# Two groups' norm sums a bunch later, a fourth raw-weight buffer, a split interval and a reordered opening in a hybrid decoder trunk

## The chip, the core and the metric

The kernel runs on one core of one Trainium2 chip. The metric is the device time of one execution in microseconds (us). Three executions of the kernel before took 1676.26, 1678.35 and 1680.52 us; the median is 1678.35 us. The engines are named as the profile names them: PE (TensorE, matmuls), PEld (its weight loads), DVE (VectorE), ACT (ScalarE), POOL (GpSimd) and SP (SyncE, which issues the DMAs). Each engine works through its own queue in order and waits at an instruction until what it needs is there.

## The reference

A trunk of four pre-norm residual layers on 512 tokens of width 1024 in float32: dilated windowed attention, a gated conv-FFN, a Mamba-2 SSD mixer, a second conv-FFN, and a final norm. The change touches the opening norm with the first attention products, and the SSD mixer:

```python
def rmsnorm(x, w):
    y = xf * lax.rsqrt(jnp.mean(xf * xf, axis=-1, keepdims=True) + NORM_EPS)
...
def ssd_mixer(h, w_in, conv_w, conv_b, dt_bias, a_log, d_skip, norm_w, w_out):
    zxbcdt = h @ w_in
    z, xbc, dt_raw = ...
    xbc = jax.nn.silu(causal_depthwise_conv(xbc, conv_w, conv_b))
    xs, bm, cm = ...
    y = ssd_chunked_scan(xs, dt, a, bm, cm)
    y = y + d_skip.astype(jnp.float32)[:, None] * xs
    y = gated_group_rmsnorm(y.reshape(bsz, s, SSM_D_INNER), z, norm_w, SSM_GROUPS)
    return y.astype(h.dtype) @ w_out
...
def gated_group_rmsnorm(y, z, w, groups):
    g = y.astype(jnp.float32) * jax.nn.silu(z.astype(jnp.float32))
    g = g.reshape(shp[:-1] + (groups, shp[-1] // groups))
    g = g * lax.rsqrt(jnp.mean(g * g, axis=-1, keepdims=True) + NORM_EPS)
```

The mixer has 32 heads of 64 channels in 8 groups of 4 heads; the scan goes in chunks of 128 tokens, and the gated norm is taken over the 256 channels of a group.

## The kernel before

**Products.** Every float32 product is made of three matmuls on numbers split into a high and a low part (`long_product`, L127). `load_unit` (L109 to 120) brings a unit of weights: one DMA into a raw buffer (pool `wr`, 3 buffers), the cast to the high part (`hi_...`) on ACT at L118, and the difference to the low part (`lo_...`) on DVE, for some units on POOL, at L119. A raw buffer is free again when the low part is made. PSUM is shared out in three rings: `mm` with 3 banks, `aux` with 3 and `side` with 2. A product that comes round to a bank waits until the tile that lay in it three turns before was read.

**Order.** PE's order in the SSD is the order of the code (`groups` runs under a manual schedule of PE). The other engines' orders come from a scheduler that sees the whole program. A change of code order on PE so moves DVE's and ACT's queues as well.

**Norms.** `inv_rms` sums squares over partitions with thin matmuls (`ss`, L196), takes mean plus epsilon on DVE (`ms`, L201) and the power -1/2 on POOL (`rcol` or `rg`, L202). `along_free` (L208) spreads the result back along the tokens with matmuls (`rb` in the opening, `prg` in a group).

**Opening.** The squares of x are summed while the first tiles of V are multiplied (`v_steps(1, 0)`, steps `first[0]` to `first[3]`). Then come `inv_rms`, `rb`, and the second half of tile products (`v_steps(2, 0)`). The scheduler chose the places of `ss` among the products of `first[3]`.

**SSD groups.** For each of 8 groups `scan_group` yields five bunches of work:

- S0: `xdt` by token (`px`, `pb` are transposes), `pc`, and `cb` (`pc` times the causal mask)
- S1: the chunk states `pst` from `xdd` (made on POOL at L679), and the decays `lm`, four of 128x512 in a group: DMA of rows, subtraction on DVE (L711), exp on ACT (L715), times `cb` on POOL (L716)
- S2: the products `py`, `pf` with `lm`, and the outputs `yt` on DVE (L746 to 751) with the gate `usz`
- S3: the sum of squares `ss`, then `ms` and `rg`
- S4: `prg`, `yt` times `prg` (DVE, L788), and its parts `y..h` (ACT), `y..l` (DVE)

`behind(g)` takes three turns: S0 of group g with S3 of group g-1, S1 of g with S4 of g-1, S2 of g. After each turn one list of `between(g)` fills PE: projections for the next groups (`x0`, `b`, `c`, `x1`, `z0`, `z1`; on PE the products `xs`, `b`, `c`, `xs`, `z`, `z` of 24 matmuls each) and steps of the output projection `wso` (`w01`, `w23`, `w4`, `w56`), whose bank DVE adds to the residual (`xr`, L812). For the last group, 7, the lists are: the eight steps of `w4`; `z1` and two steps of `w56`; two more steps.

On ACT the exp of the decays and the silu of the gates and convolutions use different tables; a change from one to the other shows as ACT_TABLE_LOAD.

## Time and profile before

| | |
|---|---|
| median of three executions | 1678.35 us |
| profiled execution, whole | 1678.73 us |
| its span on the core | 1676.9 us |
| PE idle in the span | 23.6 us (1676.9 less 1653.3 busy) |
| DVE, ACT, POOL busy | 64%, 40%, 28% of the span |
| DMA | 165.56 MB, mean 99 GB/s |

The span runs from the first to the last instruction on the core; the profiled execution's time stands 1.8 us above it. "Busy" counts time in which an engine runs an instruction; a wait is idle time in front of an instruction, and the view of waits names what ended it. In rows of the timeline the first number is the start in us from the span's start and the second how long the row lasts; "x8" says that eight alike stand in one row, and brackets give the idle time ahead of it and what ended that. In rows of the windows view each engine has its busy time and in brackets its number of instructions; "PEclk" (the column after POOL) is the granted clock of PE as a share of full speed.

### The profile page before, as it was taken

What the parts mean: (1) busy time and instruction counts of PE and PEld (TensorE: products, weight loads), DVE (VectorE), ACT (ScalarE), POOL (GpSimd) and SP (SyncE); (2) the same over time, 40 slices, a digit from 0 to 9 for tenths busy, and PEclk for the clock granted to TensorE, in tenths of its full rate; (3) what the DMA queues carried; (4) which work ended last, traced back from release to release, by engine and by line L of the source; (5) the groups of instructions that cost most, each with busy time, mean ns of one, the idle gap of its engine ahead of it and who ended that gap; (6) DMA issues with size and microseconds to landing.
All of it is one profiled execution on the core that took longest, in us unless ns stands there. A gap on an engine that the chain in (4) does not pass through costs nothing.

```text
span 1676.9 us, 21508 instructions
## 1 busy us (share of the span) xinstructions
PE 1653.3 (99%) x8230; PEld 1405.4 (84%) x8230; DVE 1073.8 (64%) x1796; ACT 671.9 (40%) x1004; POOL 468.6 (28%) x303
## 2 busy tenths in 40 slices
PE   9999999999999999999999989999989999999997
PEld 7888888888888888888888877888878888888887
DVE  5366564366657745745657878787786684574565
ACT  5233332333344423423445554344552542342345
POOL 0443443144413211211242222333221341121023
PEclk9999999999999999999999999999999999999999
DMA  6322222222223223223234322313321232332323
GB/s 226 106 83 76 80 84 88 88 85 79 76 93 134 97 86 107 101 89 113 75 102 134 101 88 89 111 65 114 113 95 64 100 106 85 112 101 89 109 75 131
DMA packets 52342, 165.56 MB, mean 99 GB/s; under 512 B 5840, under 2 KB 8144, under 8 KB 52240
## 3 DMA queue, kind: packets, MB, share of 16 engines
q1 hardware_dynamic: 51152, 163.15, 29.0%
q8 instruction: 65, 1.06, 0.3%
q10 hardware_dynamic: 1088, 1.05, 0.2%
q14 instruction: 37, 0.30, 0.1%
HBM read 162.01 MB, written 2.16 MB: 98 GB/s over the span
## 4 chain that ended last, share of the span: by engine, by line
PE 89%; DVE 4%; issue 2%; POOL 2%; ACT 1%; DMA 1%; SPq 0%; POOLq 0%; ACTq 0%; DVEq 0%
PE u L127 28%; PE qk L127 15%; PE wd L127 12%; PE v L127 6%; PE wso L127 5%; PE z L127 4%; PE xs L127 4%; PE wz L127 2%; PE b L127 2%; PE wo L127 2%; PE c L127 1%; PE pp L410 1%; PE pg L423 1%; POOL lm L716 1%; PE po L418 1%
## 5 line engine op out<-in xcount | busy, mean ns | idle before, releaser
L127 PE MATMUL u<-xh,hi_u 128*128 128x512 f32 x704 | 270.3, 384 | 0.0
L127 PE MATMUL u<-xl,hi_u 128*128 128x512 f32 x704 | 270.1, 384 | 0.2 <-DVE xl L176 0.2
L127 PE MATMUL u<-xh,lo_u 128*128 128x512 f32 x704 | 270.0, 383 | 0.0
L545 POOL TENSOR_TENSOR au<-au,au 128x512 f32<-128x512 f32 x43 | 56.7, 1318 | 427.1 <-DVE au L523 405.9
L118 ACT CAST hi_u<-raw_u 128x1024 fp32r<-128x1024 f32 x88 | 91.1, 1043 | 196.1 <-PE u L127 101.8
L523 DVE SCALAR_TENSOR_TENSOR au<-usu,par,au 128x510 f32<-128x510 f32 (+1 forms) x176 | 160.9, 919 | 5.9 <-ACT au L521 1.0
L325 POOL TENSOR_TENSOR rotqk<-rotqk,sr 32x512 f32<-32x512 f32 x48 | 91.8, 1913 | 257.5 <-DVE rotqk L324 214.4
L127 PEld LDWEIGHTS u<-xl,hi_u 128*128 128x128 f32 x704 | 131.9, 187 | 25.8 <-DVE xl L176 0.6
L127 PEld LDWEIGHTS u<-xh,lo_u 128*128 128x128 f32 x704 | 131.9, 187 | 25.3
L127 PEld LDWEIGHTS u<-xh,hi_u 128*128 128x128 f32 x704 | 131.9, 187 | 25.1
L127 PE MATMUL qk<-xh,hi_qk 128*128 128x512 f32 x384 | 149.1, 388 | 0.0
L127 PE MATMUL qk<-xl,hi_qk 128*128 128x512 f32 x384 | 148.2, 386 | 0.0
L127 PE MATMUL qk<-xh,lo_qk 128*128 128x512 f32 x384 | 147.1, 383 | 0.0
L538 DVE TENSOR_TENSOR usu<-u,rbc 128x512 f32<-128x512 f32 x88 | 60.5, 690 | 112.6 <-PE u L127 103.3
L119 DVE TENSOR_TENSOR lo_u<-raw_u,hi_u 128x1024 fp32r<-128x1024 f32 x88 | 109.6, 1252 | 24.7 <-ACT hi_u L118 24.7
L558 DVE TENSOR_TENSOR xr<-xr,wd 128x512 f32<-128x512 f32 x40 | 27.2, 686 | 116.6 <-PE wd L127 116.6
L321 DVE TENSOR_TENSOR qk<-qk,cr 128x512 f32<-128x512 f32 x48 | 33.0, 687 | 91.0 <-PE qk L127 90.8
L118 ACT CAST hi_qk<-raw_qk 128x1024 fp32r<-128x1024 f32 x48 | 50.1, 1044 | 101.8 <-PE v L127 50.8
L127 PEld LDWEIGHTS qk<-xh,lo_qk 128*128 128x128 f32 x384 | 72.0, 188 | 13.3
L118 ACT CAST hi_wd<-raw_wd 128x1024 fp32r<-128x1024 f32 (+1 forms) x56 | 52.4, 951 | 76.2 <-PE wd L127 39.7
L127 PEld LDWEIGHTS qk<-xh,hi_qk 128*128 128x128 f32 x384 | 72.0, 188 | 12.8
L127 PEld LDWEIGHTS qk<-xl,hi_qk 128*128 128x128 f32 x384 | 72.1, 188 | 12.4
(637 smaller groups left out, 3954.1 us busy)
## 6 DMA issues: line engine op xcount, KB each, us to landing
raw_u<-in_wup SPq DMA_DIRECT2D x88, 512.0 KB, 3.2
raw_qk<-in_wqk SPq DMA_DIRECT2D x48, 512.0 KB, 3.2
raw_wd<-in_wdn SPq DMA_DIRECT2D x32, 512.0 KB, 3.2
raw_wd<-in_wdn SPq DMA_DIRECT2D x24, 384.0 KB, 3.0
raw_xs<-in_win SPq DMA_DIRECT2D x16, 512.0 KB, 3.3
raw_z<-in_win SPq DMA_DIRECT2D x16, 512.0 KB, 3.6
lm<-rows SPq DMA_DIRECT2D x32, 256.0 KB, 4.9
raw_wso<-in_wso SPq DMA_DIRECT2D x16, 512.0 KB, 3.3
```

The source lines that it names most:

```text
L118: SC.copy(hi[:, s], raw[:, s])
L119: low.tensor_tensor(lo[:, s], raw[:, s], hi.bitcast(F32)[:, s], op=ALU.subtract)
L127: T.matmul(in_turns(dst), w, in_turns(x), start=first, stop=last)
L321: V.tensor_tensor(at(t), of(p), of(cr), op=ALU.mult)
L325: G.tensor_tensor(rot[R, :], rot[R, :], sr[R, :], op=ALU.mult)
L410: T.transpose(pp[:, b * P : (b + 1) * P], pr[:, b * P : (b + 1) * P], ident)
L418: T.matmul(po[:, ii], v0[h][:, b * P : (b + 1) * P], pts[i][:, (b - i + 1) * P : (b - i + 2) * P], start=b == max(i - 1, 0), stop=b == i,)
L423: T.matmul(pg[:, ii], vt[g, half][i][:, es], pts[i][:, (g + 1) * P : (g + 2) * P], start=g == 1, stop=g == 2,)
L523: V.scalar_tensor_tensor(dst[:, j:], src[:, : S - j], col(c_w + taps - 1 - j), dst[:, j:], op0=ALU.mult, op1=ALU.add,)
L538: V.tensor_tensor(us, p, rbc, op=ALU.mult)
L545: by.tensor_tensor(ab[1], ab[0], ab[1], op=ALU.mult)
L558: V.tensor_tensor(xr[m], xr[m], p, op=ALU.add)
```

## The change

- Raw weights get a fourth buffer (`wr`, 3 to 4). To make room, `lm` has 4 buffers where it had 5, and `cb` 1 where it had 2.
- A step of `v_steps` can be asked for one half of its unit.
- In the opening, PE's order is written out: the first half of `first[3]`, `ss`, the second half, `rb`. DVE's order there is written out too: `ms`, and behind it the low parts of the first unit of `v_steps(2, 0)`, which is now loaded ahead.
- In `behind(g)` for g = 1 and 2, S3 of the group before comes with S1 of g (behind `pst`) and S4 with S2 of g (ahead of `py`). From g = 3 on it stays as it was. `prg` takes an `aux` bank.
- In group 7 the first list is four steps of `w4` and `z1`; the second is the other four steps and two of `w56`.

No engine has an arithmetic instruction more or less than before.

```diff
-    wr = ctx.enter_context(tc.tile_pool(name="wr", bufs=3))
+    wr = ctx.enter_context(tc.tile_pool(name="wr", bufs=4))
...
-        def step(u):
+        def step(u, bs=(0, 1)):
...
-                for b in range(2):
+                for b in bs:
...
-    inv_rms(ssum, D, rcol)
-    first[3]()
-    rb = along_free(rcol, "rb")
+    load2, second = v_steps(2, 0)
+    with tc.manual_schedule(engines={mybir.EngineType.PE}):
+        first[3]((0,))
+        with tc.manual_schedule(engines={mybir.EngineType.DVE}):
+            inv_rms(ssum, D, rcol)
+            load2(0)
+        first[3]((1,))
+        rb = along_free(rcol, "rb")
...
-                t = t2("lm", "lm", 5, lp)
+                t = t2("lm", "lm", 4, lp)
...
-        cb = t2("cb", "cb", 2, lp)
+        cb = t2("cb", "cb", 1, lp)
...
-        prg = along_free(rg, "prg", side_bank)
+        prg = along_free(rg, "prg")
...
         for i in range(3):
+            late = g in (1, 2)
+            if late and i == 2:
+                next(scans[g - 1], None)
             next(scans[g])
-            if g and i < 2:
+            if g and i == (1 if late else 0) or g > 2 and i == 1:
                 next(scans[g - 1], None)
             yield
...
-        return w4, [ahead[g][5], *w56[:2]], w56[2:4]
+        return [*w4[:4], ahead[g][5]], [*w4[4:], *w56[:2]], w56[2:4]
```

What it does to the queues is seen at three places. In the opening PE had `ss` in the midst of `v_138`, with products of a low part behind it that belong to the first half:

```order
L127 MATMUL v_138<-hi_v_252,xh_89 128x4x32x4
L127 MATMUL v_138<-hi_v_252,xl_97 128x4x32x4
L196 MATMUL ss<-ones,ssum 128x1 x4
L127 MATMUL v_138<-lo_v_253,xh_89 128x4x32x4
L127 MATMUL v_139<-lo_v_253,xh_88 128x4x32x4
L127 MATMUL v_139<-hi_v_252,xh_89 128x4x32x4
L127 MATMUL v_139<-hi_v_252,xl_97 128x4x32x4
L127 MATMUL v_139<-lo_v_253,xh_89 128x4x32x4
L127 MATMUL v_140<-lo_v_253,xh_88 128x4x32x4
L127 MATMUL v_140<-hi_v_252,xh_89 128x4x32x4
L127 MATMUL v_140<-hi_v_252,xl_97 128x4x32x4
L127 MATMUL v_140<-lo_v_253,xh_89 128x4x32x4
```

Nine products lay between `ss` and `rb` there; now the same place on PE is:

```order
L127 MATMUL v_140<-lo_v_253,xh_88 128x4x32x4
L196 MATMUL ss<-ones,ssum 128x1 x4
L127 MATMUL v_137<-hi_v_252,xh_89 128x4x32x4
L127 MATMUL v_137<-hi_v_252,xl_97 128x4x32x4
L127 MATMUL v_137<-lo_v_253,xh_89 128x4x32x4
L127 MATMUL v_138<-hi_v_252,xh_89 128x4x32x4
L127 MATMUL v_138<-hi_v_252,xl_97 128x4x32x4
L127 MATMUL v_138<-lo_v_253,xh_89 128x4x32x4
```

The other six products of `v_139` and `v_140` follow and then `rb`: twelve, the whole second half, now stand between `ss` and `rb`.

In group 2, DVE had `yt` times `prg` between two rows of the convolution `ac`, far ahead of the outputs:

```order
L694 TENSOR_TENSOR prev<-prev,cdec 128x128
L788 SCALAR_TENSOR_TENSOR yt<-yt,par,prg 128x512 x2
L698 TENSOR_TENSOR prev<-prev,pst 128x128
L523 SCALAR_TENSOR_TENSOR ac_7953<-usc_7951,par,ac_7953 128x510
L698 TENSOR_TENSOR prev<-prev,pst 128x128
L792 TENSOR_TENSOR y10l<-yt,y10h 128x512
```

Now it stands behind the first `usz` (`z0` of the next group), right ahead of the outputs of this one:

```order
L648 TENSOR_TENSOR usz_8093<-z_8068,rbc 128x512
L793 SCALAR_TENSOR_TENSOR yt<-yt,par,prg 128x512 x2
L119 TENSOR_TENSOR lo_b_8307<-raw_b_8305,hi_b_8306 128x1024
L797 TENSOR_TENSOR y10l<-yt,y10h 128x512
L797 TENSOR_TENSOR y11l<-yt,y11h 128x512
L716 TENSOR_SCALAR lm<-lm,acs 128x128
L751 TENSOR_TENSOR ee<-ee,pf 128x384
```

A few rows on, the gate of `z1` (`usz_8183`), for whose bank the next `xs` on PE waits, has come in among the rows of `lm`, which before stood all ahead of it:

```order
L755 TENSOR_TENSOR yt<-yt,ee 128x384 x2
L756 TENSOR_TENSOR yt<-yt,usz_7715 128x512
L756 TENSOR_TENSOR yt<-yt,usz_7805 128x512
L716 TENSOR_SCALAR lm<-lm,acs 128x128 x6
L648 TENSOR_TENSOR usz_8183<-z_8158,rbc 128x512
L716 TENSOR_SCALAR lm<-lm,acs 128x128 x6
```

The four operations on `prg` (2.8 us of DVE work, at the durations that the same rows have in the trace: two of 0.70 and two of 0.68 us) have moved down behind the convolutions, and the last `usz` has moved up. On ACT the silu of that gate now parts the exps of the decays two and two, with a table load on each side of it.

In group 7 ACT's queue had, from the decays' first exp on:

```order
L708 ACTIVATE ee<-lm 64x384 x4
L649 ACT_TABLE_LOAD
L649 ACTIVATE axs_9821<-axs_9821 128x512
L118 CAST hi_z_10120<-raw_z_10119 128x1024
L753 ACTIVATE gsq<-yt 128x512 x2
L715 ACT_TABLE_LOAD
L715 ACTIVATE lm<-lm 128x512 x3
L645 ACT_TABLE_LOAD
L645 ACTIVATE usz_9899<-usz_9899 128x512
L715 ACT_TABLE_LOAD
L715 ACTIVATE lm<-lm 128x512
L118 CAST hi_wso_10154<-raw_wso_10153 128x1024
```

Now it has, at the same place:

```order
L654 ACTIVATE axs_9827<-axs_9827 128x512
L713 ACT_TABLE_LOAD
L713 ACTIVATE ee<-lm 64x384 x4
L758 ACTIVATE gsq<-yt 128x512
L118 CAST hi_wso_10122<-raw_wso_10121 128x1024
L758 ACTIVATE gsq<-yt 128x512
L720 ACTIVATE lm<-lm 128x512 x4
L650 ACT_TABLE_LOAD
L650 ACTIVATE usz_9905<-usz_9905 128x512
L118 CAST hi_wso_10160<-raw_wso_10159 128x1024
L118 CAST hi_wso_10166<-raw_wso_10165 128x1024
```

Three of the four table loads behind the first exps are gone, and the cast of a unit for `z1` stands further up; the unit that is `hi_wso_10154` before is `hi_wso_10160` now.

More of the change, by code (lines that the diff above doesn't have):

```diff
@@ L252, in step @@
                 js = slice(j * P, (j + 1) * P)
-                for b in range(2):
+                for b in bs:
                     k = 2 * u + b
-                    bs = slice(b * 512, (b + 1) * 512)
+                    cs = slice(b * 512, (b + 1) * 512)
                     p = state["p"][j]
-                    long_product(p, xh[k][:, js], hi[:, bs], k == 0, False)
-                    long_product(p, xl[k][:, js], hi[:, bs], False, False)
-                    long_product(p, xh[k][:, js], lo[:, bs], False, k == KD - 1)
-            if u == 3:
+                    long_product(p, xh[k][:, js], hi[:, cs], k == 0, False)
+                    long_product(p, xl[k][:, js], hi[:, cs], False, False)
+                    long_product(p, xh[k][:, js], lo[:, cs], False, k == KD - 1)
+            if u == 3 and bs[-1]:
                 tiles = []
@@ L266, in step @@
                 vt[g, half] = tiles
-        return load, [lambda u=u: step(u) for u in range(4)]
+        return load, [lambda *bs, u=u: step(u, *bs) for u in range(4)]
     ssum = t2("ssum", "ssum", 2)
@@ L303, in trunk @@
     dma(tri, A["tri"])
-    for f in v_steps(2, 0)[1]:
+    for f in second:
         f()
```

## Prediction

> **What bounds the kernel now.** I begin with the page's first part, the busy time of each engine, and its fourth, the chain that ended last:

> ```profile
> PE 1653.3 (99%) x8230; PEld 1405.4 (84%) x8230; DVE 1073.8 (64%) x1796; ACT 671.9 (40%) x1004; POOL 468.6 (28%) x303
> PE 89%; DVE 4%; issue 2%; POOL 2%; ACT 1%; DMA 1%; SPq 0%; POOLq 0%; ACTq 0%; DVEq 0%
> ```

> PE is busy for 99% of the span. No arithmetic is taken away, so the change can only win what PE loses in idle time and at a lowered clock. The view of PE's waits says where:

> ```profile
> PE prg L208 <- POOL rg L202: 6.7, 2, 4.4
> PE wso L127 <- DVE xr L812: 4.9, 1, 4.9
> PE rb L208 <- POOL rcol L202: 1.7, 1, 1.7
> ```

> These are total, count and longest in us: two waits of `prg` (4.40 and 2.31), one of `wso`, one of `rb`, 13.3 us together. The change aims at all four. Behind each I look at the granted clock, in the windows view:

> ```profile
> 972.03:978.03 6.00, 6.00 (x18) 5.13 (x19) 4.91 (x10) 3.79 (x7) 0.00 (x0) 0.50 0.26 87
> 1018.40:1024.40 6.00, 6.00 (x24) 5.07 (x25) 4.91 (x10) 3.79 (x7) 0.00 (x0) 0.72 0.25 87
> 1254.13:1260.00 5.87, 5.87 (x18) 4.68 (x19) 4.01 (x5) 1.05 (x1) 5.87 (x5) 0.66 0.30 94
> 27.00:33.00 6.00, 4.26 (x23) 3.35 (x23) 2.54 (x4) 4.46 (x7) 1.02 (x1) 1.00 0.81 270
> ```

> The number behind POOL's is the granted clock. Behind the waits of `prg` and `wso` it is 0.50, 0.72 and 0.66: PE is "busy", yet loses 6.00 x 0.50 = 3.0, 6.00 x 0.28 = 1.7 and 5.87 x 0.34 = 2.0 us. Around the 1.74 us of `rb` it stays at 1.00. So the four places cost 1.7 + (4.4 + 3.0) + (2.3 + 1.7) + (4.9 + 2.0) = 20.0 us. That is the most that the change can win.

> **The opening.** The rows, in order of time:

> ```profile
> 25.23 0.95 PE L196 MATMUL ss<-ones,ssum 128*128 128x1 f32 x8
> 27.55 1.23 DVE L119 TENSOR_TENSOR lo_v<-raw_v,hi_v 128x1024 fp32r<-128x1024 f32 x1 [1.46 <-ACT hi_v L118]
> 27.95 0.38 PE L127 MATMUL v<-lo_v,xh 128*128 128x512 f32 x1
> 28.70 0.15 DVE L201 TENSOR_SCALAR ms<-ss 128x4 f32<-128x4 f32 x1
> 29.00 1.02 POOL L202 TENSOR_TENSOR rcol<-ms,mhalf 128x4 f32<-128x4 f32 x1 [28.56 <-DVE ms L201]
> 30.07 1.16 PE L208 MATMUL rb<-ident,rcol 128*128 128x128 f32 x8 [1.74 <-POOL rcol L202]
> ```

> `ss` ends at 26.18, yet `ms` starts at 28.70, since DVE stands at a low part that waits for ACT. From `ms` to `rb` it takes 30.07 - 28.70 = 1.37 us. With `ms` right behind `ss` (DVE's order is written so), `rcol` is there some 1.4 us after `ss`. Twelve products cover this: the last started at 27.95, two microseconds behind `ss`, with nine. The wait goes whole: -1.7. What DVE pays is that the four low parts start behind `ms`; four of 1.23 from 25.7 end at 30.6 instead of 28.8. PE takes up the first of them only behind `rb`, at about 29.3, with two low parts made by then, and the next ones no sooner than some six products (1.3 us) apart: covered. Without that cover the price is the 1.8 us that the last of them is late, and the term is zero. Bounds -1.7 and 0.

> **Groups 1 and 2.** Three rows of group 1 and three of the end of group 2:

> ```profile
> 962.99 0.15 DVE L201 TENSOR_SCALAR ms<-ss 128x4 f32<-128x4 f32 x1
> 963.72 6.85 POOL L716 TENSOR_TENSOR lm<-lm,cb 128x512 f32<-128x512 f32 x4
> 970.52 1.45 POOL L202 TENSOR_TENSOR rg<-ms,mhalf 128x4 f32<-128x4 f32 x1
> 1041.71 2.63 DVE L711 TENSOR_SCALAR lm<-lm,acs 128x128 f32<-128x128 f32 x13
> 1044.87 0.68 DVE L643 TENSOR_TENSOR usz<-z,rbc 128x512 f32<-128x512 f32 x1
> 1045.78 0.38 PE L127 MATMUL xs<-xh,hi_xs 128*128 128x512 f32 x1
> ```

> The first three rows show why `prg` waits: `ms` is ready at 963.1, but POOL does the four `lm` first, and only then `rg`. POOL's order isn't changed. What changes is that PE asks for `prg` only ahead of `py`, two projections of 24 products (11 us) later; and `py` needs these `lm` anyway. So the wait at its old place is gone: -4.4 - 3.0 and -2.3 - 1.7, together -11.4.

> But PE is not alone near its limit there. The windows from `cb` of group 1 to the last `usz` of group 2, and two groups further on without a wait:

> ```profile
> 959.56:1045.47 85.91, 79.19 (x425) 67.29 (x424) 69.69 (x124) 39.34 (x61) 27.91 (x17) 0.94 0.28 92
> 1102.69:1154.40 51.71, 51.71 (x285) 44.16 (x284) 42.07 (x69) 24.15 (x36) 14.92 (x9) 1.00 0.31 103
> 1154.40:1206.00 51.60, 51.60 (x298) 44.53 (x297) 43.86 (x73) 24.42 (x36) 17.69 (x13) 1.00 0.31 103
> ```

> In the first, DVE is busy 69.69 us (the third engine). If PE ran free, the stretch would last 85.91 - 11.4 = 74.5, and DVE would have to be busy for 94% of it. In the groups without waits, DVE is at 42.07 / 51.71 = 81% and 43.86 / 51.60 = 85%. DVE's queue is in order and stands now and then for ACT, POOL and DMA, so I take 85% as what it reaches: 69.69 / 0.85 = 82.0 us, and the gain is 85.91 - 82.0 = **3.9** of 11.4.

> Where would the rest come back? At the next thing that DVE owes PE. The last two rows of the first fence show the tightest: the bank of `z1` was read by `usz` from 1044.87 to 1045.55, and PE's `xs` takes it at 1045.78, with 0.2 us to spare. PE comes there up to 11 us earlier; DVE's `usz` has moved ahead of 13 - 6 = 7 `lm` rows (2.63 / 13 = 0.20 each, 1.4 us) but stands behind the four `prg` operations, which came down the queue. Two smaller waits come with it: `ms` now stands in DVE's queue behind the convolution `ac`, and `xdd` on POOL behind casts on ACT. ACT pays two table loads more in each group, since the silu of `z1` now stands between the exps: 4 x 1.28 = 5.1 us (a row of one is below), on an engine at 24.15 / 51.71 = 47%. If these were all on the path, with nothing gained, the term would be +5.1; the other end is -11.4, and I take -3.9.

> **Group 7.** PE, DVE and ACT around its wait:

> ```profile
> 1235.92 2.17 ACT L708 ACTIVATE ee<-lm 64x384 f32<-64x384 f32 x4 [3.89 <-DVE yt L750]
> 1240.88 1.15 ACT L753 ACTIVATE gsq<-yt 128x512 f32<-128x512 f32 x2
> 1242.04 1.28 ACT L715 ACT_TABLE_LOAD   x1
> 1243.34 1.67 ACT L715 ACTIVATE lm<-lm 128x512 f32<-128x512 f32 x3
> 1246.32 0.63 ACT L645 ACTIVATE usz<-usz 128x512 f32<-128x512 f32 x1
> 1248.80 1.98 ACT L118 CAST hi_wso<-raw_wso 128x1024 fp32r<-128x1024 f32 x2
> 1248.85 0.38 PE L127 MATMUL wso<-y41h,lo_wso 128*128 128x512 f32 x1
> 1249.86 1.23 DVE L119 TENSOR_TENSOR lo_wso<-raw_wso,hi_wso 128x1024 fp32r<-128x1024 f32 x1 [4.68 <-ACT hi_wso L118]
> 1253.41 1.87 DVE L812 TENSOR_TENSOR xr<-xr,wso 128x512 f32<-128x512 f32 x3
> 1254.13 0.79 PE L127 MATMUL wso<-y40h,hi_wso 128*128 128x512 f32 x1 [4.91 <-DVE xr L812]
> ```

> PE has done three steps of `w4` by 1249; the fourth needs the bank of the first, which DVE adds to `xr` only at 1253.41, behind a low part that waits for ACT's cast at 1248.80. The split puts `z1` behind the **fourth** step, so the fourth still asks for the same bank at the same time. What helps is another thing: ACT's queue (shown with the change). Behind the first exps, which end at 1238.09, it now has two `gsq` (1.15), a cast (1.0), four `lm` (1.67 / 3 x 4 = 2.2), a table load (1.28), `usz` (0.63) and then the cast: 6.3 us, and the convolution's silu ahead of it all (0.63). The cast would end at 1238.1 + 0.6 + 6.3 + 1.0 = 1246.0 instead of 1249.83. From that low part's start to `xr` DVE needs 1253.41 - 1249.86 = 3.6 us and one `xdt` more (0.6, which before lay ahead). PE could go on at 1246.0 + 4.2 + 0.7 = 1250.9, 3.2 us sooner. This asks that ACT waits for nothing, while its row of 1235.92 shows that it does; between 0 and 3.2 I take two thirds, **-2.1**. Bounds: 0, and -6.9 if the wait vanished with its clock loss.

> **The fourth raw buffer, and the smaller `lm` and `cb`.** No wait of PE names a weight DMA, so an earlier load wins nothing. `cb` is read by POOL's `lm` long before the next group's `cb`. Four `lm` buffers are just one group's: the next group's DMAs start when `py` has read the last. Zero for all three; what it costs where cover is lost is in the third rival.

> **Sum**: -1.7 - 3.9 - 2.1 = -7.7. The profiled execution took 1678.73 us, 0.4 above the median of the runs: 1678.73 - 7.7 = **1671.0 us**.

> [...]

> [...]

> **Rivals.** *Everything is won.* DVE's busy time in the window holds rows that ran long beside POOL, and if PE's new place eases that, DVE can follow. It gives -20.0: 1658.7 at best, and some 1663 when only the DVE-bound stretch follows and group 7 is as in the forecast (-1.7 - 11.4 - 2.1 = -15.2). Against it stands 94% of DVE. Chance 0.2.

> *The waits come back whole.* DVE holds 81%, as in the window at 1102.69, and not 85%: 69.69 / 0.81 = 86.0, no gain in groups 1 and 2; in group 7 the split does not do what it says, since `xr` of the first step is where it was. Only the opening counts: 1677.0. Chance 0.25.

> [...] PE comes to `prg`, `xs` of the next group and `pst` earlier, and DVE and ACT are late for each: in both groups one `prg` wait and one bank wait as long as the worst in the trace, 4.4 + 3.0 and 4.9 + 2.0, so 28.6 in place of 11.4: +17.2, with the opening and group 7 +13.4, so 1692. It needs a DVE that falls behind by more than the idle time that was removed. It is slower than before as soon as the new waits come to more than 11.4 + 3.8 = 15.2 us, and it would be measured as such above 20. The table loads with the silu between exps, and the `lm` DMAs that all start behind `py`, speak for it; against it stands that DVE's work is the same. Chance 0.1.

> *The shortened wait keeps the clock.* In group 7 the wait that is left, 2.8 us, lies between the 1.74 that kept 1.00 and the 4.9 that lost 2.0 us; the one of 2.31 lost 1.7. If 2.8 lost nothing, the time would be 1671.0 - 2.0 = 1669.0. Since the 2.31 lost, it has 0.05, inside the forecast's range. [...]

> **How the numbers follow.** The forecast has 0.40, with the rival of the kept clock 0.45. Its own range is 1667 to 1676. The limit of what a measurement of this kernel can tell from no change is 0.3%, here 5.0 us: faster lies below 1673.3, slower above 1683.4. Of these 0.45 I put 0.34 below 1673.3; all 0.2 of the first rival; 0.03 of the second: faster 0.57. Slower is 0.08 of the third rival and 0.01 of the second: 0.09. The rest, 0.34, is the same. The range from 1660 to 1680 leaves out the far end of the first rival and most of the third.

> **What would show it.** In the waits of PE, `rb <- rcol` is gone, and `ms` of the opening stands right behind `ss`. `prg <- rg` at the old place is gone in both groups. In its stead, `xs` or `wso` waits for DVE's `usz` or `xr`, and PE's clock drops there, or (the first rival) neither is seen and DVE is above 90% in the two groups. `wso <- xr` in group 7 is still there, 2 to 3 us long, and shorter by what ACT's cast came sooner. I am wrong if DVE runs the window at other than 85%, if `prg` waits ahead of `py` for a late `ms`, or if a wait turns up in the opening behind `rb`.

## The result, and the profile after

Six executions of the changed kernel took 1666.9 to 1673.19 us, median 1669.41; six of the kernel before took 1676.26 to 1680.52, median 1678.54. The ratio is 0.995 with a 95% interval of 0.9933 to 0.9967: faster by 5.5 to 11.2 us. The forecast was 1671.0, in a range of 1660 to 1680. A second set of the same two kernels, on another occasion (`again`, below), gave 1668.94 and a ratio of 0.9948 (0.9932 to 0.9963).

The profiled execution after took 1667.39 us, 11.3 less than the one before. Its page and its view of PE's waits:

```profile
PE 1648.4 (99%) x8230; PEld 1400.9 (84%) x8230; DVE 1076.4 (65%) x1796; ACT 669.9 (40%) x1004; POOL 466.9 (28%) x303
PE 89%; DVE 6%; ACT 2%; issue 1%; DMA 1%; POOL 0%; SPq 0%; POOLq 0%; ACTq 0%; DVEq 0%
...
PE wso L127 <- DVE xr L817: 2.9, 1, 2.9
PE xs L127 <- DVE usz L648: 2.8, 3, 1.9
...
PE prg L208 <- POOL rg L202: 0.9, 1, 0.9
```

The wait of `rb` for `rcol` is gone, the two of `prg` are one of 0.9, that of `wso` is 2.9 instead of 4.9, and three new ones of `xs` for `usz` make 2.8. So 13.3 us of waits have become 6.6. PE's busy time fell too, by 4.9 us (1653.3 to 1648.4), though it does the same matmuls: most of this is the lowered clock that is no longer there (a loss of 3.0 + 1.7 + 2.0 us before, by the rows in the prediction, and of 1.5 now). In the windows view, from group 1's first `axs` beside `cb` to group 2's last `usz`, then behind the new waits of `prg`, `xs` and `wso`, the granted clock (behind POOL's number) is

```profile
957.48:1035.16 77.68, 75.02 (x429) 63.96 (x427) 68.45 (x117) 39.62 (x59) 26.84 (x17) 1.00 0.31 102
1018.11:1024.11 6.00, 6.00 (x60) 5.46 (x61) 5.43 (x11) 2.28 (x3) 0.00 (x0) 1.00 0.30 103
1035.29:1041.29 6.00, 6.00 (x30) 5.17 (x31) 4.46 (x11) 5.94 (x9) 0.00 (x0) 1.00 0.27 87
1243.44:1249.31 5.87, 5.87 (x20) 4.89 (x21) 3.59 (x4) 1.05 (x1) 5.87 (x5) 0.74 0.17 71
```

The first row answers to 85.91 us before. Only behind `wso` is the clock still lowered: 5.87 x 0.26 = 1.5 us, where it was 2.0.

**Where the time went**, by what PE starts in both traces. The `px` of group 1 came at 951.83 and now comes at 950.27: 1.6 us. The `xs` behind the new wait in group 2 came at 1045.78, now at 1035.29: 10.5, so 8.9 in groups 1 and 2. By the `ss` in group 7 (1244.04 and 1235.27) 8.8 is left, so groups 3 to 6 gave back 1.7. The `pst` of group 7 came at 1262.87, now at 1251.60: 11.3, so 2.5 in group 7. Nothing is won or lost behind it. This is one execution against one, and the one after lies 2.0 us below its median; what the other traces say of each size stands in the section on the prediction.

The timeline's rows behind these numbers, first the opening:

```profile
23.84 0.95 PE L196 MATMUL ss<-ones,ssum 128*128 128x1 f32 x8
24.82 0.16 DVE L201 TENSOR_SCALAR ms<-ss 128x4 f32<-128x4 f32 x1 [3.38 <-PE ss L196]
24.90 4.62 DVE L119 TENSOR_TENSOR lo_v<-raw_v,hi_v 128x1024 fp32r<-128x1024 f32 x4
25.13 1.86 POOL L202 TENSOR_TENSOR rcol<-ms,mhalf 128x4 f32<-128x4 f32 x1 [24.69 <-DVE ms L201]
27.40 1.05 PE L208 MATMUL rb<-ident,rcol 128*128 128x128 f32 x8
```

`ms` now follows `ss` at once, the four low parts stand behind it without a gap, and `rb` finds `rcol` ready. `rcol` took 1.86 us beside DVE's low parts where it had taken 1.02 with DVE idle for most of it; the twelve products cover that too. Next group 2 (and `ms` and `rg` of group 1 in the first two rows):

```profile
973.76 0.15 DVE L201 TENSOR_SCALAR ms<-ss 128x4 f32<-128x4 f32 x1
973.99 1.01 POOL L202 TENSOR_TENSOR rg<-ms,mhalf 128x4 f32<-128x4 f32 x1 [5.46 <-DVE ms L201]
1016.81 0.15 DVE L201 TENSOR_SCALAR ms<-ss 128x4 f32<-128x4 f32 x1
1018.11 1.16 PE L208 MATMUL prg<-ident,rg 128*128 128x128 f32 x8 [0.92 <-POOL rg L202]
1034.56 0.68 DVE L648 TENSOR_TENSOR usz<-z,rbc 128x512 f32<-128x512 f32 x1
1035.29 0.48 PE L127 MATMUL xs<-xh,hi_xs 128*128 128x512 f32 x1 [1.88 <-DVE usz L648]
```

It isn't POOL's `lm` any more that hold `rg` back but `ms`, which stands behind DVE's convolution: POOL waits 5.46 us for it in group 1 and PE 0.92 in group 2. Last, group 7, on ACT, DVE and PE:

```profile
1229.28 2.16 ACT L713 ACTIVATE ee<-lm 64x384 f32<-64x384 f32 x4
1235.67 1.28 ACT L650 ACT_TABLE_LOAD   x1
1237.50 1.98 ACT L118 CAST hi_wso<-raw_wso 128x1024 fp32r<-128x1024 f32 x2
1238.56 1.23 DVE L119 TENSOR_TENSOR lo_wso<-raw_wso,hi_wso 128x1024 fp32r<-128x1024 f32 x1 [2.15 <-ACT hi_wso L118]
1242.70 1.87 DVE L817 TENSOR_TENSOR xr<-xr,wso 128x512 f32<-128x512 f32 x3
1243.44 0.80 PE L127 MATMUL wso<-y40h,hi_wso 128*128 128x512 f32 x1 [2.94 <-DVE xr L817]
```

From the end of the exps `ee` (1231.44) to the cast is 6.1 us, where it was 10.7; four table loads have become one.

### The profile page after: what moved, and what is told of

Same layout as the page of the kernel before. It is cut to its first block, busy times and chain, and to the rows that moved or that the text cites. A ratio compares the mean times of both kernels' runs of the same rounds, so it can differ in the third digit from the quotient of the medians.

```text
span 1665.6 us, 21514 instructions
## 1 busy us (share of the span) xinstructions
PE 1648.4 (99%) x8230; PEld 1400.9 (84%) x8230; DVE 1076.4 (65%) x1796; ACT 669.9 (40%) x1004; POOL 466.9 (28%) x303
## 3 DMA queue, kind: packets, MB, share of 16 engines
q8 instruction: 65, 1.06, 0.3%
q10 hardware_dynamic: 1088, 1.05, 0.2%
HBM read 162.01 MB, written 2.16 MB: 99 GB/s over the span
## 4 chain that ended last, share of the span: by engine, by line
PE 89%; DVE 6%; ACT 2%; issue 1%; DMA 1%; POOL 0%; SPq 0%; POOLq 0%; ACTq 0%; DVEq 0%
PE u L127 28%; PE qk L127 15%; PE wd L127 12%; PE v L127 8%; PE xs L127 4%; PE wso L127 4%; PE z L127 3%; PE b L127 2%; PE wz L127 2%; PE c L127 2%; PE wo L127 2%; DVE axs L528 1%; PE pp L415 1%; PE pg L428 1%; PE po L423 1%
## 5 line engine op out<-in xcount | busy, mean ns | idle before, releaser
L127 PE MATMUL u<-xl,hi_u 128*128 128x512 f32 x704 | 270.1, 384 | 0.4 <-DVE xl L176 0.4
L127 PE MATMUL u<-xh,hi_u 128*128 128x512 f32 x704 | 270.3, 384 | 0.0
L127 PE MATMUL u<-xh,lo_u 128*128 128x512 f32 x704 | 270.0, 384 | 0.0
L118 ACT CAST hi_u<-raw_u 128x1024 fp32r<-128x1024 f32 x88 | 91.1, 1043 | 194.0 <-PE u L127 102.2
L127 PEld LDWEIGHTS u<-xl,hi_u 128*128 128x128 f32 x704 | 131.9, 187 | 25.9 <-DVE xl L176 0.8
L127 PEld LDWEIGHTS u<-xh,lo_u 128*128 128x128 f32 x704 | 131.9, 187 | 25.3
L127 PEld LDWEIGHTS u<-xh,hi_u 128*128 128x128 f32 x704 | 131.9, 187 | 25.2
L127 PE MATMUL qk<-xh,hi_qk 128*128 128x512 f32 x384 | 149.4, 389 | 0.0
L127 PE MATMUL qk<-xl,hi_qk 128*128 128x512 f32 x384 | 148.4, 386 | 0.0
L127 PE MATMUL qk<-xh,lo_qk 128*128 128x512 f32 x384 | 147.3, 384 | 0.0
L119 DVE TENSOR_TENSOR lo_u<-raw_u,hi_u 128x1024 fp32r<-128x1024 f32 x88 | 110.8, 1264 | 24.2 <-ACT hi_u L118 24.2
L118 ACT CAST hi_qk<-raw_qk 128x1024 fp32r<-128x1024 f32 x48 | 50.1, 1045 | 100.4 <-PE v L127 49.9
L127 PEld LDWEIGHTS qk<-xh,lo_qk 128*128 128x128 f32 x384 | 72.0, 187 | 13.5
L118 ACT CAST hi_wd<-raw_wd 128x1024 fp32r<-128x1024 f32 (+1 forms) x56 | 52.3, 950 | 76.7 <-PE wd L127 39.7
L127 PEld LDWEIGHTS qk<-xh,hi_qk 128*128 128x128 f32 x384 | 72.0, 188 | 13.0
L127 PEld LDWEIGHTS qk<-xl,hi_qk 128*128 128x128 f32 x384 | 72.1, 188 | 12.5
```

Of the source, the lines that this page charges most:

```text
L118: SC.copy(hi[:, s], raw[:, s])
L119: low.tensor_tensor(lo[:, s], raw[:, s], hi.bitcast(F32)[:, s], op=ALU.subtract)
L127: T.matmul(in_turns(dst), w, in_turns(x), start=first, stop=last)
```

## The experiments

All ratios are to the kernel before, run on the same chip beside each, with 95% intervals. Four kernels make one edit alone on the kernel before; eight start from the changed kernel.

**Opening alone** (`open_only`): only the part of the change on `v_steps` and the opening.

```diff
...
+        first[3]((0,))
+        with tc.manual_schedule(engines={mybir.EngineType.DVE}):
+            inv_rms(ssum, D, rcol)
+            load2(0)
+        first[3]((1,))
...
```

> The kernel before with the new opening alone. Theory: the wait of rb for rcol (1.74 us) goes whole and nothing comes back, so -1.7 us against before; rb starts no later than the last product of the second half ends. Rival (DVE's low parts behind ms are late): rb is earlier but a product of the second V half waits, net 0 to -0.5 us. In the profiled pair the opening was 2.8 us shorter 20 us on; if that is of the change, -2.7 us.

1675.06 us, ratio 0.9986 (0.9977 to 0.9994), so 1.0 to 3.9 us. No wait of `rb` for `rcol`, and no product of the second half of V waits. `rb` starts at 27.79, where it was 30.07. The term holds, but its size is a matter of the execution: in the three kernels that follow, whose opening code is that of before, the same wait was 1.33, 0.94 and 0.46 us:

```profile
30.05 1.16 PE L208 MATMUL rb<-ident,rcol 128*128 128x128 f32 x8 [1.33 <-POOL rcol L202]
```

(`late_only`), and in `split_only` and `bufs_only`

```profile
29.98 1.16 PE L208 MATMUL rb<-ident,rcol 128*128 128x128 f32 x8 [0.94 <-POOL rcol L202]
...
28.45 1.16 PE L208 MATMUL rb<-ident,rcol 128*128 128x128 f32 x8 [0.46 <-POOL rcol L202]
```

The last has the fourth raw buffer, so it isn't quite the opening of before.

**Sums and scale later, alone** (`late_only`):

```diff
-        prg = along_free(rg, "prg", side_bank)
+        prg = along_free(rg, "prg")
...
-            if g and i < 2:
+            if g and i == (1 if late else 0) or g > 2 and i == 1:
```

> The kernel before with the sums and scale of groups 0 and 1 one bunch later, nothing else. Theory (each wait has its own latency, DVE has room): the two prg waits and their clock loss go (-11.4 us), the xs behind z1 in group 2 waits some 2 us for usz, so PE is 8 to 10 us earlier at the end of group 2, and the whole is -7 to -9 us. Rival (DVE's throughput is the bound at 85% busy, as forecast): -4 us, DVE no more than 85% busy from cb of group 1 to the last usz of group 2.

1672.32 us, ratio 0.9968 (0.9957 to 0.998), so 3.4 to 7.2 us, 4.6 by the medians: less than the 7 to 9 of the theory, and by the time alone it could be either. The profile tells more. Its window over the same stretch, and its waits for `usz`:

```profile
960.29:1038.21 77.92, 74.67 (x427) 63.59 (x425) 68.52 (x116) 39.62 (x59) 26.82 (x17) 1.00 0.30 102
```

```profile
PE xs L127 <- DVE usz L643: 3.5, 2, 2.1
```

DVE was busy 68.52 / 77.92 = 88% and not 85%, and the stretch was 8.0 us shorter than in the profile before, not 3.9. Part of the 8.0 is that profile's own bad luck: `open_only` (first row) and `split_only` have the old order in these groups, and took 81.78 and 84.46 us over the same stretch, not 85.91.

```profile
958.35:1040.13 81.78, 75.71 (x423) 64.68 (x422) 69.51 (x124) 39.70 (x61) 27.93 (x17) 0.98 0.28 97
960.23:1044.69 84.46, 78.14 (x425) 66.45 (x424) 69.55 (x124) 39.34 (x61) 27.93 (x17) 0.96 0.27 94
```

So the gain in the stretch is 3.9 to 8.0 us, by the execution that it is held against. Against that stand the new waits for `usz`, 2.1 and 1.4 us in groups 2 and 3. That `prg` takes another bank was not tried apart from its place.

**Split alone** (`split_only`):

```diff
-        return w4, [ahead[g][5], *w56[:2]], w56[2:4]
+        return [*w4[:4], ahead[g][5]], [*w4[4:], *w56[:2]], w56[2:4]
```

> The kernel before with the split of group 7 alone. Theory (the gain there is ACT's, whose queue loses its parted table loads, while the fourth step still waits for the first step's bank): the wait of wso for xr is still there, 2.5 to 3.5 us, with the clock at 0.7 behind it, and the whole is -2 to -3 us. Rival (z1 between the halves hides the wait): no wait of wso for xr, -6.9 us.

1675.13 us, ratio 0.9981 (0.9973 to 0.999), so 1.7 to 4.5 us. The wait is there:

```profile
PE wso L127 <- DVE xr L812: 3.7, 1, 3.7
```

ACT's exps stand together in this kernel, as in the changed one. The rival, that `z1` hides the wait, is out; the 3.7 lie a little above what was expected.

**Buffers alone** (`bufs_only`):

```diff
+    wr = ctx.enter_context(tc.tile_pool(name="wr", bufs=4))
...
+                t = t2("lm", "lm", 4, lp)
...
+        cb = t2("cb", "cb", 1, lp)
```

> The kernel before with the fourth raw buffer, four lm and one cb alone. Theory: no wait of PE names a weight DMA, so 0 within 1.5 us. Rival (part of the gain is earlier loads): the waits of prg and wso get shorter by more than 1 us in all, -2 us or more.

1675.89 us, ratio 0.9992 (0.9983 to 1.0): from nothing to 2.9 us. `prg` waited 5.7 instead of 6.7 and `wso` 4.7 instead of 4.9, 1.2 in all. This lies between the two theories; no wait of PE names a weight DMA in it, so the second isn't shown.

**Split taken back** (`no_split`): the changed kernel with the first two lists of group 7 as before.

> The changed kernel with the first two lists of group 7 as before (w4 whole, then z1). Theory: ACT's queue has its parted table loads back, so DVE's low part and the xr behind it come later and the wait of wso for xr is 4 to 5 us again where the changed kernel has 2.9; +2 to +3 us against the changed kernel (1669.4). Rival (the gain in group 7 is only what the earlier edits gave): wait 2.9 us, no difference.

1671.76 us, ratio 0.9954 (0.9937 to 0.9971). PE waited 4.7 us for `xr`, as expected. The 2 to 3 us in time are not shown: 2.4 by the medians, but 0.7 by the ratios (0.9954 here, 0.995 for the changed kernel, which was not run beside this one). ACT's table loads behind the exps, and the first cast of `wso` behind them:

```profile
1231.27 1.28 ACT L654 ACT_TABLE_LOAD   x1
1235.21 1.28 ACT L720 ACT_TABLE_LOAD   x1
1237.67 1.28 ACT L650 ACT_TABLE_LOAD   x1
1239.61 1.28 ACT L720 ACT_TABLE_LOAD   x1
1241.44 1.03 ACT L118 CAST hi_wso<-raw_wso 128x1024 fp32r<-128x1024 f32 x1
```

Between the end of `ee` (1229.09 + 2.16 = 1231.25) and this cast lie 10.2 us, nearly as much as before the change (10.7), against 6.1 in the changed kernel. With the loads the wait came back. No run changes ACT's order alone, so that the loads made the wait is read from this chain.

**`z1` behind the third step** (`split3`):

```diff
-        return [*w4[:4], ahead[g][5]], [*w4[4:], *w56[:2]], w56[2:4]
+        return [*w4[:3], ahead[g][5]], [*w4[3:], *w56[:2]], w56[2:4]
```

> The changed kernel with z1 behind the third step of w4 instead of the fourth. Theory (the bank decides, whatever product comes fourth): z1 takes the bank that the first step left, and z waits for xr as long as wso did, 2.5 to 3.5 us; no difference to the changed kernel. Rival (z1's 5.4 us cover the wait once they stand ahead of the waiting step): no wait, clock at 1.00, -4.4 us.

1670.98 us, ratio 0.9948 (0.9931 to 0.9964). Now `z` waits, for the same bank and as long:

```profile
1246.34 0.80 PE L127 MATMUL z<-xh,hi_z 128*128 128x512 f32 x1 [2.99 <-DVE xr L817]
```

**`z1` behind the third step, in an aux bank** (`z1_aux`):

```diff
-        return [*w4[:4], ahead[g][5]], [*w4[4:], *w56[:2]], w56[2:4]
+        return [*w4[:3], ahead[g][5], w4[3]], [*w4[4:], *w56[:2]], w56[2:4]
...
-            lambda: d.update(z1=ssm_tile(i + 5, None, f"z{g}1")),
+            lambda: d.update(z1=ssm_tile(i + 5, None, f"z{g}1", aux_bank if g == NSG - 1 else mm_bank)),
```

> The changed kernel with group 7's z1 behind the third step of w4, as in split3, but in an aux bank, so that no product ahead of the fourth step needs the first step's bank; ACT's queue keeps its exps together. Theory (the bank decides): z1 runs at once, the fourth step comes 5.4 us later and finds its bank read, so no wait of z or wso over 0.5 us in group 7 and no clock loss: -4 to -4.5 us there. Rival (DVE is so late that anything there waits): a wait of 2 us or more at z1, the fourth step, pst or prg; less than 2 us gained.

1666.24 us, ratio 0.9931 (0.9919 to 0.9943), 2.7 below the changed kernel beside it. Neither `z` nor the fourth step waits; the fourth starts at 1248.10, and `xr` of the first has begun at 1245.16. PE reached `pst` at 1249.43, against 1252.98 in `again`, and from `ss` of group 7 to it took 11.7 us against 16.4: 4.7 less, as the theory has it. One wait of `wso` for `xr` of 0.5 us came up behind, and in this execution the short wait of `xs` in group 2, 1.9 us, cost clock (0.72 over the 6 us behind it), which it did not in `again` (1.00).

**`z1` ahead of the four steps** (`z1_first`):

```diff
-        return [*w4[:4], ahead[g][5]], [*w4[4:], *w56[:2]], w56[2:4]
+        return [ahead[g][5], *w4[:4]], [*w4[4:], *w56[:2]], w56[2:4]
```

> The changed kernel with z1 ahead of the first four steps of w4. The step that needs the first step's bank comes 5.4 us later on PE, but the scheduler puts the parted table loads back on ACT (three more of 1.28 us ahead of the cast). Theory (the wait is the later of ACT's chain and PE): the wait of wso is 0 to 1.5 us and PE's clock stays at 0.9 or more, -2 to -4 us against the changed kernel. Rival (ACT's four loads cost all that z1 covers): wait 2 to 4 us, no difference.

1668.93 us, ratio 0.9938 (0.9923 to 0.9953). Three short waits instead of one, of 1.78, 0.85 and (at 1260.12, behind `pst`) 0.60 us, the clock at 1.00 behind the first two:

```profile
1247.83 0.49 PE L127 MATMUL wso<-y40h,hi_wso 128*128 128x512 f32 x1 [1.78 <-DVE usz L648]
1250.28 0.49 PE L127 MATMUL wso<-y40h,hi_wso 128*128 128x512 f32 x1 [0.85 <-DVE xr L817]
```

The first was not foreseen: with `z1` in the ring, the third step needs the bank of `z1`. The sum, 3.2 us, lies in the rival's range: four table loads are back on ACT behind the exps, and PE gains 1.6 us from `ss` of group 7 to `pst` against `again` and loses 1.4 behind it.

**`xs` ahead of `wso` in group 2** (`xs_first`):

```diff
-                [[b, c], [x1, z0], [z1, *w01[:2], after]],
+                [[b, c], [x1, z0], [z1, after, *w01[:2]]],
```

> The changed kernel with the xs of group 4 ahead of the two wso steps in the third list of group 2, so that xs needs not z1's bank and usz gets 5.5 us more. Theory (one bank's latency): the wait of xs for usz in group 2 (1.9 us) is gone and nothing takes its place, PE 1.5 to 2 us earlier at the px behind it. Rival (DVE's throughput is the bound): the same 1.5 to 2 us come back at the next things that DVE owes (prg, pst, xs of the next group), 0 by the end of group 3.

1667.08 us, ratio 0.9929 (0.9915 to 0.9944). The wait in group 2 is gone, and those behind it have grown: `prg` waits 0.23 in group 3, `xs` 1.65 there and 0.90 in group 4, where the changed kernel had 0.54 and 0.34.

```profile
1057.54 1.16 PE L208 MATMUL prg<-ident,rg 128*128 128x128 f32 x8 [0.23 <-POOL rg L202]
...
1087.89 0.46 PE L127 MATMUL xs<-xh,hi_xs 128*128 128x512 f32 x1 [1.65 <-DVE usz L648]
...
1140.71 0.46 PE L127 MATMUL xs<-xh,hi_xs 128*128 128x512 f32 x1 [0.90 <-DVE usz L648]
```

Of 1.88 us, 1.1 + 0.6 + 0.2 = 1.9 came back in this trace, as the rival had it. The times do not bear this out: the ratio is lower than the changed kernel's (0.995 and 0.9948) and the same as that of `xs_all` below, but the changed kernel was not run beside this one, and the profiled execution (1668.61) is the slowest of its four. What stayed open was whether it must come back, or only finds the next tight bank.

**`xs` ahead of `wso` in groups 2, 3 and 4** (`xs_all`): the same edit in three lists.

> The changed kernel with xs ahead of the two wso steps in the third lists of groups 2, 3 and 4. Theory (DVE fell behind in groups 1 and 2 and catches up in groups 3 to 6, where it is 81 to 85% busy, if no bank is asked of it too early): none of the waits of xs for usz (2.8 us in the changed kernel) is left, -2 to -3 us by the end of group 4. Rival (the debt must be paid whatever the order): prg, ss, pst or wso waits take their place in groups 3 to 5, less than 1 us gained.

1666.46 us, ratio 0.9929 (0.9915 to 0.9943), 2.5 below the changed kernel beside it. No wait for `usz` is left, and `prg` has two waits of 1.1 us in all. The window over the stretch of groups 1 and 2:

```profile
958.13:1035.80 77.67, 76.75 (x438) 65.80 (x437) 68.45 (x116) 39.61 (x59) 26.83 (x17) 1.00 0.30 102
```

DVE takes the same 77.7 us for its part of the two groups as in the changed kernel, and is busy the same 68.45; but PE's busy time in it is 76.75 instead of 75.02. PE's waits don't set DVE's pace there, and PE doesn't have to wait for it as long as no bank is asked of it too early. The waits show this; the time in part only, since the profiled execution (1663.94) is the fastest of its five and its wait of `wso` in group 7, 2.94 us, cost no clock (1.00 over the 6 us behind it; last section).

**Both** (`best`): the edits of `z1_aux` and `xs_all`.

> The edits of z1_aux and xs_all together on the changed kernel. If both theories hold, the sum: -6 to -7 us against the changed kernel, about 1662 to 1663 us. If only one holds, -2.5 or -4.4 us. If the debt of DVE is moved on to group 7, less than the better of the two.

1662.39 us (1662.06 to 1662.99), ratio 0.9907 (0.9893 to 0.9921): 16.7 us below the kernel before and 6.5 below the changed one beside it. What PE still waits for in the SSD:

```profile
PE prg L208 <- POOL rg L202: 1.1, 2, 0.9
PE ss L196 <- DVE gsq L786: 1.1, 1, 1.1
```

The wait of `ss`, in group 7, is longer than the 0.5 of the changed kernel, and the clock went down behind it (0.72 over 6 us, 1.7 us lost). Whether DVE's debt has moved on to group 7 with it is open.

**The changed kernel again** (`again`):

> The changed kernel itself, on the same chip as the three others. Theory: 1669 us within 2 us, ratio 0.995; the waits for usz in groups 2 to 4 and of wso for xr in group 7 as before, 2.8 and 2.9 us within 0.5. Rival (these waits are chance of one execution, as rb's proved to be): one of them shorter by 1 us or more.

1668.94 us, ratio 0.9948 (0.9932 to 0.9963); `wso` waited 3.0 us for `xr` and `xs` 2.9 for `usz`. These waits belong to the kernel, not to one execution.

## Why the prediction was right, and where its size was off

**What bounds, and where.** Right. The four places that were named are where the time came from, and in the profiled pair nothing else moved by more than 2 us. The four parts run alone won 1.8 (opening), 4.6 (groups 1 and 2), 1.8 (group 7) and 1.0 us (buffers) by their medians, 9.1 in all; so did the whole change, where 7.7 were forecast.

**The opening, -1.7.** The mechanism is shown by `open_only`. The price is that of one execution: the same wait was 0.94 and 1.33 us in others with the same opening. In the profiled pair it looked larger, 2.7 us at `rb`, but by group 1 only 1.6 was left. In between PE kept a slightly faster pace in the trace before (192 matmuls against 190 in 40 us; last section). Over all traces the first `px` of group 1 comes at 951.8 to 952.5 us in the three with the old opening and buffers, and at 950.3 to 951.4 in the ten with the new opening: 1.4 between the means.

**Groups 1 and 2, -3.9.** This is the term that was mis-sized, by less than the profiled pair says: that pair gives 8.9 us, less the 1.7 that groups 3 to 6 gave back, so 7.2. From `px` of group 1 to `ss` of group 7 the three traces with the old order and buffers took 289.4 to 292.2 us, the seven with the new order and the old place of `xs` 285.0 to 286.8: 4.9 between the means, as `late_only` has it (4.6). The step that failed is "I take 85% as what it reaches". In the stretch DVE reached 68.45 / 77.68 = 88%; and it had 1.2 us less to do (69.69 before), since seven rows fewer fall into it (117, not 124), a low part of 1.2 us among them. So it lasted 77.7 us and not 82.0. That the total came as near as it did is in part luck: the stretch came out 4.3 us below the forecast, but the 85.91 from which the term was reckoned is the longest of three traces. And there was a second error in the same step: it took DVE's time for PE's. `xs_all` shows that DVE's stretch is 77.7 us with or without PE's wait; PE may run ahead of it by as much as its banks allow, and in `xs_all` no wait for `usz` comes back in groups 3 to 6.

The wait that was forecast, `xs` for `usz`, came, 1.88 us long; the lowered clock behind it did not (1.00). The smaller wait that was named with it, `ms` late behind `ac`, came too: `prg` 0.92. So of the three signs by which the prediction would be wrong two were seen, DVE at 88% and `prg` waiting ahead of `py` for a late `ms`; the first is the failed step, the second cost 0.9 us. The third, a wait behind `rb` in the opening, was not seen. The added table loads cost no time of PE that any run shows.

**Group 7, -2.1.** Right in mechanism and size: 2.5 in the pair; and from `ss` to `pst` 18.8 to 19.3 us in five traces with the old lists and 16.3 to 17.2 in four with the split whose wait cost clock. The wait stayed at the fourth step, as forecast at 2.8 us and found at 2.94, since it needs the first step's bank (`split3` moved the wait onto `z`, `z1_aux` took it away by another bank), and it got shorter with ACT's table loads (`no_split` brought both back). The working put the cast 6.3 us behind the exps; it was 6.1.

**Buffers, 0.** Not settled: `bufs_only` gave nothing to 2.9 us, with its two waits shorter by 1.2 in all. Why the `prg` wait came out shorter there was not tried.

**The rivals.** "Everything is won" fell for this change, but DVE, named against it, was not what forbade it: with the two edits of `best`, which take the remaining bank waits away, the gain is 16.7 of the 20.0 us that had been named as the most. "The waits come back whole" and the slower one fell with the waits that were seen: in groups 1 to 4 the new ones made 0.9 + 2.8 us, against the 15.2 from which the slower one would have begun. "The shortened wait keeps the clock" fell in the profiled execution (0.74 behind `wso`, 1.5 us) and in three more traces with a wait of 2.9 to 3.7 us at this place (0.72 in `split_only` and `xs_first`, 0.73 in `again`), but held in that of `xs_all` (1.00 behind 2.94 us): the last section shows how the two waits of 2.94 us lie on the grid.

## What to carry to other kernels

Where PE waits for a bank, count which product in the ring meets it, and give the engine that reads the bank more products in between, or another bank; a list split behind that product leaves the wait where it is. Moving work from one engine's tight spot changes the queues of the others: here what the split won came, as far as the traces show, from a queue that it put in better order. When a second engine is near its limit over a stretch, it doesn't follow that the first must take as long: look at how far ahead it may run, and if the second has room later to catch up.

## What the runs showed of the hardware that was not expected

```profile
1034.08:1037.49 3.41, 1.57 (x8) 1.02 (x7) 3.41 (x13) 3.31 (x7) 0.00 (x0) 1.00 0.00 0
1037.49:1040.91 3.42, 3.42 (x10) 2.65 (x9) 3.42 (x8) 3.39 (x5) 0.00 (x0) 0.50 0.17 19
...
1236.77:1240.18 3.41, 1.58 (x8) 0.99 (x6) 3.41 (x5) 0.93 (x2) 1.75 (x2) 1.00 0.41 144
1240.18:1243.59 3.41, 2.31 (x10) 1.99 (x11) 2.91 (x6) 0.89 (x1) 3.41 (x4) 1.00 0.47 163
1243.59:1247.00 3.41, 3.41 (x17) 2.85 (x16) 1.24 (x2) 0.17 (x1) 3.41 (x3) 1.00 0.25 72
```

PE got through 10 instructions in the lowered cell of `split3` and 17 in the last one of `xs_all`; over the 6 us behind the gap in `split3` the clock is 0.72, a price of 6 x 0.28 = 1.7 us. In the traces before and after, between the opening and the last 14 us, all five cells with 2.0 us or more of idle time (2.03 to 3.41) were followed by a lowered one, and of the full-speed cells with less (1.41 at most) none was. Behind waits of 1.8 to 1.9 us in group 2 the clock over 6 us was 0.72 in `split3`, `z1_aux` and `split_only`, but 1.00 in `again`, `no_split` and `z1_first`; behind one of 2.15 in `late_only` it was 1.00 too. In `best` a wait of `ss` of 1.06 us, in a cell with the eight thin matmuls of `ss` in it, was enough:

```profile
1232.06:1235.47 3.41, 2.35 (x15) 1.95 (x15) 2.40 (x4) 3.38 (x6) 0.00 (x0) 1.00 0.45 153
1235.47:1238.88 3.41, 3.41 (x10) 2.64 (x9) 2.27 (x3) 2.43 (x4) 0.30 (x1) 0.50 0.04 7
```

So idle time is not all that counts: 1.06 us in a cell were enough here, 1.41 in a cell of the trace after were not. What else does is open. The ten gaps of 3.7 us and more all cost clock (0.50 to 0.73 over the 6 us behind them). From these numbers a wait of 2 us has an estimated price of 2 or of nearly 4 (2 + 1.7), by whether the clock goes down behind it. It may be why six executions of the changed kernel spread over 6.3 us and four of `best` over 0.9; but five of `late_only`, which has waits of 2.1 and 1.4 us, spread over 1.3 us, so this isn't shown.

Also at a granted clock of 1.00 PE's pace isn't always the same. In 40 us without a wait, ahead of the SSD's groups, the window holds 192 matmuls before and 190 after:

```profile
860.00:900.00 40.00, 40.00 (x192) 34.09 (x191) 25.94 (x41) 19.93 (x26) 12.33 (x7) 1.00 0.32 106
```

```profile
860.00:900.00 40.00, 40.00 (x190) 33.61 (x189) 26.67 (x43) 20.52 (x27) 10.53 (x6) 1.00 0.32 106
```

From `rb` to the first `px` of the SSD it is 882.6 us before and 883.8 after. This is not of the change: `late_only`, with the code of before there, has 190 in this window as well. It is where part of the opening's gain went in the profiled pair; what makes it is open.
